# Stick-breaking attention: eight heads one by one, or four pairs of heads with two heads in an instruction

## The chip, the cores and the metric

The kernel runs on one core of one Trainium2 chip. TensorE (PE) multiplies, with its weight load (PEld) beside it; VectorE (DVE) and ScalarE (ACT) work on what it leaves in PSUM; GpSimd (POOL) and the DMA queues (SP's above all) do the rest. The metric is the device time of one execution in microseconds, the median of several.

## The reference

Two transformer blocks stand one behind the other, each on 512 tokens of width 1024. The first has stick-breaking attention and a gated recurrence side by side, and then a mixture of 16 experts; the second has retention, differential attention, cross attention and a feed-forward layer. The change touches the stick-breaking attention alone. It has 8 heads of width 64, and computes for a head

```
z           = (q k^T) / 8                                  # 512 queries x 512 keys
mask        = key position < query position
log_keep    = where(mask, log_sigmoid(-z), 0)
log_survive = reverse cumulative sum over keys of log_keep, shifted by one
a           = where(mask, exp(log_sigmoid(z) + log_survive), 0)
out         = a v
```

Since log_sigmoid(z) = z - softplus(z) and log_sigmoid(-z) = -softplus(z), the exponent is z minus the sum of softplus(z) over this key and all later keys that the query sees.

## The kernel before, in words

All wide products (a projection by a weight matrix) are made exact to fp32 by three products of rounded halves: `mm3` (L186 to L189) multiplies hi by hi, hi by lo and lo by hi. A weight tile of 512 KB comes in on SP's queue, ACT rounds it to `whi` (L169), DVE subtracts to `wlo` (L170), and 24 products of 128x512 make one output tile of 128 columns for all tokens. There are three buffers for the raw tile, and four for each half.

Scores are held transposed, keys on the partitions and queries along the row. A block j is 128 keys against the queries from 128 j on, so its width is n = 512, 384, 256 or 128 for j = 0 to 3. The head's steps (`sb_head`, L606) are: the score product of each block, plus a product of the identity with `negsb` that adds -1e30 where a query must not see the key (L615, L616); DVE copies the scores to `z` (L617); ACT makes exp(-|z|) and log(1 + that) in three passes, Abs, Exp and Ln (L619 to L621); DVE adds max(z, 0) (L622), which gives softplus; ACT and DVE split it into the halves `ph` and `pl` (L253, L254). Then, for each block, products with a triangle of ones (`tri`) and with all ones (`onesr`) over this block and the later ones give the sum over later keys (L633, L634); DVE subtracts it from z (L636), ACT takes the exponential (L637), and the product with the values goes into the head's half of `ysbp` (L638). ACT and DVE split that into `ysb`.

The q of a head stands in a tile of 128 partitions whose other 64 are zero, so that a score product runs over all 128 partitions. PSUM has eight banks: two of tag "mm" for the wide products, two of "tp", and four of "at", which scores and sums share. An fp32 product shows two records in the trace, a product of halves (fp32r) one.

A scheduler sets each engine's order when the kernel is built, and an engine then works strictly in that order. Around the eight heads it interleaves the wide products of the gates (16 tiles, L656 and L657, copied out by L653), which depend on the heads in nothing; their tiles share the 21 slots of `slp` with q, k and v, and five more (`GX`). After the last gate the branch products begin, the first of them with `ysb`.

Retention, in the second block, already has the form that the change gives to the attention here: `ret_pair` (L1256) multiplies the k and q of two heads on partitions 0 to 63 and 64 to 127 (L1266), and the values of two heads into the two halves of one PSUM tile (L1271).

Of the kernel before, what the change touches and what calls it, by code (L numbers as in the profile page):

```python
# [8 lines left out]
F32 = mybir.dt.float32  # L9
F32R = mybir.dt.float32r  # L10
# [3 lines left out]
AF = mybir.ActivationFunctionType  # L14
OP = mybir.AluOpType
AX = mybir.AxisListType.X
PSUM = bass.MemoryType.PSUM
# [3 lines left out]
S = 512  # L21
# [4 lines left out]
HID = 2816  # L26
CAP = 96
OVER = 10
NSL = 21
GX = (5, 6, 7, 8, 9)  # L30
NRX = 8
NRX2 = 12

# [50 lines left out]
def body(tc, a, out):  # L84
    nc = tc.nc
    V, A, T, G = nc.vector, nc.scalar, nc.tensor, nc.gpsimd
    es = ExitStack()

    def pool(name, bufs, side=None, space=None, stack=None):
        kw = {}  # L90
        if side:
            kw["side"] = side
        if space is not None:
            kw["space"] = space
        return (stack or es).enter_context(tc.tile_pool(name=name, bufs=bufs, **kw))
# [9 lines left out]
    hp = pool("hp", 1)  # L105
    ps = pool("ps", 1, space=PSUM)
    dp = pool("dp", 1, space=DRAM)

    def psum(tag, name="ps"):
        return ps.tile([128, 512], F32, name=name, tag=tag, bufs={"mm": 2, "at": 4, "tp": 2}[tag])  # L110

    def new_hT():
        return (hp.tile([128, 8, S], F32R, name="hTh"), hp.tile([128, 8, S], F32R, name="hTl"))
# [138 lines left out]
    def hilo(hi, lo, src):  # L252
        A.copy(hi, src)  # L253
        last_lo[:] = [V.tensor_sub(lo, src, hi.bitcast(F32))]  # L254
# [46 lines left out]

    def sums(tag, ones, *sq):
        w = sq[0].shape[1]
        m = psum(tag)[:, :w]
        for i, q in enumerate(sq):
            T.matmul(m, ones, q, start=(i == 0), stop=(i == len(sq) - 1))  # L306
        return m
# [91 lines left out]
    at = ExitStack()  # L399
    yp = pool("yp", 1, stack=at)  # L400
    yhg = [yp.tile([128, 4, S], F32R, name=f"yhg{i}") for i in range(2)]
    ysb = [yp.tile([128, 4, S], F32R, name=f"ysb{i}") for i in range(2)]
    slp = pool("slp", 1, stack=at)

    def slot(name):
        return slp.tile([128, S], F32, name=name, tag="sl", bufs=NSL)
# [165 lines left out]

    def ev_sq(t0):
        def f(t, o):
            for h in range(2):
                q = slot("sq")
                sq_[2 * (t0 + t) + h] = q
                G.memset(q[64 - 64 * h:128 - 64 * h, :], 0.0)
                A.activation(q[64 * h:64 * h + 64, :], o[64 * h:64 * h + 64, :], AF.Copy, scale=0.125)
        return f  # L580

    def ev_sk(t0):
# [13 lines left out]
        ws(w_in, 8, 512 + t * 128, 1, hT, S, ev_sk(t))  # L596
    hgst.close()

    slp2 = pool("slp2", 1, stack=at)
    sbst = ExitStack()  # L600
    sb = pool("sb", 1, side="right", stack=sbst)
    COL = [0, 512, 896, 1152, 1280]

    last_exp = []

    def sb_head(h):  # L606
        t = h // 2
        z = sb.tile([128, 1280], F32, name="z", bufs=2)
        ph = sb.tile([128, 1280], F32R, name="ph", bufs=2)
        pl = sb.tile([128, 1280], F32R, name="pl", bufs=2)  # L610
        for j in range(4):
            n = S - 128 * j
            cc = slice(COL[j], COL[j + 1])
            o = psum("at")[:, :n]
            T.matmul(o, sk_[t][:, j * 128:(j + 1) * 128], sq_[h][:, j * 128:], start=True, stop=False)  # L615
            T.matmul(o[:, :128], identb, negsb, start=False, stop=True)  # L616
            V.tensor_copy(z[:, cc], o)  # L617
            e = sb.tile([128, S], F32, name="ea", bufs=3)[:, :n]
            A.activation(e, o, AF.Abs)  # L619
            A.activation(e, e, AF.Exp, scale=-1.0)  # L620
            A.activation(e, e, AF.Ln, bias=onec)  # L621
            V.scalar_tensor_tensor(e, z[:, cc], 0.0, e, op0=OP.max, op1=OP.add)  # L622
            hilo(ph[:, cc], pl[:, cc], e)
        y = psum("tp", name="ysbp")
        for j in range(4):
            n = S - 128 * j
            cc = slice(COL[j], COL[j + 1])
            o = psum("at")[:, :n]
            for i in range(j, 4):
                m = tri if i == j else onesr  # L630
                ci = slice(COL[i], COL[i + 1])
                oo = o[:, (i - j) * 128:]
                T.matmul(oo, m, ph[:, ci], start=(i == j), stop=False)  # L633
                T.matmul(oo, m, pl[:, ci], start=False, stop=(i == 3))  # L634
            w = sb.tile([128, S], F32, name="ea", bufs=3)[:, :n]
            V.tensor_sub(w, z[:, cc], o)  # L636
            last_exp[:] = [A.activation(w, w, AF.Exp)]  # L637
            T.matmul(y[64 * (h % 2):64 * (h % 2) + 64, 128 * j:], sv_[j][:, h * 64:(h + 1) * 64], w,  # L638
                     start=(j == 0), stop=(j == 3))
        p0 = 64 * (h % 2)  # L640
        hilo(ysb[0][p0:p0 + 64, t, :], ysb[1][p0:p0 + 64, t, :], y[p0:p0 + 64, :])

    for h in range(8):
        sb_head(h)


    gt = {}

    def ev_gate(key):
        def f(t, o):  # L650
            n = t + (8 if key == "h" else 0)
            gt[key, t] = slot("gt") if n not in GX else slp2.tile([128, S], F32, name="gt2", bufs=len(GX))
            order(A.copy(gt[key, t], o), last_sk[0])  # L653
        return f

# [758 lines left out]
    ts(a["w_down_2"][0], NH, 0, 4, aT, ev_out(0), by_token=False, tag="at")  # L1414
    ts(a["w_down_2"][0], NH, 512, 4, aT, ev_out(512), by_token=False, tag=["mm", "mm", "tp", "tp"])
    fst.close()
    xp2.close()
    kvst.close()
    es.close()
# [25 lines left out]
```

## Time and profile before

| | |
|---|---|
| median of 3 runs | 1643.37 us (1640.85 to 1863.65) |
| profiled execution | 1641.05 us, span 1639.3 us |
| PE busy | 1602.2 us, 98% of the span |
| DVE, ACT busy | 960.2 us, 833.1 us |
| heads and gates, first score to first branch product | 231.6 to 391.2 us |

A busy time of PE is not the time that its work needs: a record of a 128x512 product lasts 0.39 us, while products that follow each other start 0.23 us apart. So the text counts from start to start. A row of the timeline merges products of one line that follow each other; its second number lasts to the end of the last, some 0.16 us after a product that follows would start (0.39 less 0.23). Numbers in brackets are idle time before an instruction, and what ended it.

### The profile page before, as it was taken

The page shows a single profiled execution, that of the slowest core. Times are in us where ns is not written, and L with a number is a line of the kernel's source. Part 1 is how long each engine was busy: PE and PEld are TensorE (multiplying, and loading weights), DVE is VectorE, ACT ScalarE, POOL GpSimd, SP SyncE. Part 2 cuts the span into 40 slices and gives each one's busy share as a digit, 9 for nine tenths or more (in the row PEclk, how much of TensorE's full clock was granted, in tenths as well). Part 3 has the DMA queues.
Part 4 walks back from the last instruction along what each step waited for, and adds up shares of the span by engine and source line. Part 5 has one row for each costly group of instructions (what it writes and reads, how often), then busy time and mean ns, then how long its engine had stood idle before and what let it go on. Part 6 is the DMA issues. An engine that isn't in the chain of part 4 may idle for free. (4 is left out here: it accounts for less than half of the span.)

```text
span 1639.3 us, 20501 instructions
## 1 busy us (share of the span) xinstructions
PE 1602.2 (98%) x7663; PEld 1234.2 (75%) x7663; DVE 960.2 (59%) x1533; ACT 833.1 (51%) x1331; POOL 74.6 (5%) x92
## 2 busy tenths in 40 slices
PE   7999999999999999999999999999999999999999
PEld 6887776678878777777677667558778888888887
DVE  6459945543647999999865656456654433333221
ACT  5445557565335888888765545425444423222120
POOL 3000000000001211110010000000000000000000
PEclk9999999999999999999999999999999999999999
DMA  7230121123479999999954213124311433333241
GB/s 230 66 103 27 57 82 30 52 93 101 141 244 328 342 370 362 368 361 364 371 192 136 64 52 91 45 71 128 91 52 52 116 103 91 103 91 103 91 128 39
DMA packets 203071, 242.89 MB, mean 148 GB/s; under 512 B 10400, under 2 KB 133560, under 8 KB 202968
## 3 DMA queue, kind: packets, MB, share of 16 engines
q1 hardware_dynamic: 188800, 205.43, 37.7%
q0 software_dynamic: 7056, 24.27, 5.3%
q10 hardware_dynamic: 7112, 11.85, 2.4%
q8 instruction: 61, 1.00, 0.2%
q14 instruction: 42, 0.34, 0.1%
HBM read 223.69 MB, written 15.73 MB: 146 GB/s over the span
## 5 line engine op out<-in xcount | busy, mean ns | idle before, releaser
L170 DVE TENSOR_TENSOR wlo<-wraw,whi 128x1024 fp32r<-128x1024 f32 x210 | 256.1, 1223 | 287.2 <-ACT whi L169 277.3
L169 ACT CAST whi<-wraw 128x1024 fp32r<-128x1024 f32 x210 | 220.5, 1051 | 387.6 <-PE ps L188 263.5
L187 PE MATMUL ps<-hTh,whi 128*128 128x512 f32 (+1 forms) x912 | 349.6, 384 | 1.3 <-DVE fsg L1396 0.8
L188 PE MATMUL ps<-hTl,whi 128*128 128x512 f32 (+1 forms) x912 | 348.2, 382 | 0.9 <-DVE hTl L254 0.9
L189 PE MATMUL ps<-hTh,wlo 128*128 128x512 f32 (+1 forms) x912 | 347.5, 381 | 0.0
L170 DVE TENSOR_TENSOR wlo<-rx,whi 128x1024 fp32r<-128x1024 f32 x176 | 210.8, 1221 | 33.9 <-ACT whi L169 32.6
L169 ACT CAST whi<-rx 128x1024 fp32r<-128x1024 f32 x176 | 183.2, 1049 | 51.6 <-PE ps L189 39.1
L187 PEld LDWEIGHTS ps<-hTh,whi 128*128 128x128 f32 x912 | 172.2, 189 | 34.1 <-issue 1.5
L188 PEld LDWEIGHTS ps<-hTl,whi 128*128 128x128 f32 x912 | 172.1, 189 | 33.3 <-issue 1.6
L189 PEld LDWEIGHTS ps<-hTh,wlo 128*128 128x128 f32 x912 | 172.1, 189 | 31.8 <-issue 0.9
L187 PE MATMUL ps<-whi,XT 128*96 128x512 f32 x256 | 102.0, 398 | 1.8 <-ACTq L1032 1.8
L189 PE MATMUL ps<-whi,XT 128*96 128x512 f32 x256 | 102.5, 400 | 0.0
L188 PE MATMUL ps<-wlo,XT 128*96 128x512 f32 x256 | 101.4, 396 | 0.0
L189 PE MATMUL ps<-whi,hTl 128*128 128x512 f32 x192 | 77.2, 402 | 0.0
L187 PE MATMUL ps<-whi,hTh 128*128 128x512 f32 x192 | 76.5, 398 | 0.3 <-ACT hTh L253 0.2
L188 PE MATMUL ps<-wlo,hTh 128*128 128x512 f32 x192 | 76.6, 399 | 0.0
L187 PE MATMUL ps<-whi,aTh 128*128 128x512 f32 x176 | 68.5, 389 | 0.0
L188 PE MATMUL ps<-wlo,aTh 128*128 128x512 f32 x176 | 68.5, 389 | 0.0
L189 PE MATMUL ps<-whi,aTl 128*128 128x512 f32 x176 | 68.5, 389 | 0.0
L1396 DVE TENSOR_TENSOR fsg<-fsg,ps 128x512 f32<-128x512 f32 x22 | 15.1, 688 | 76.0 <-PE ps L189 76.0
L187 PEld LDWEIGHTS ps<-whi,XT 128*96 128x96 f32 x256 | 41.7, 163 | 18.7 <-ACTq L1032 2.2
L188 PEld LDWEIGHTS ps<-wlo,XT 128*96 128x96 f32 x256 | 41.7, 163 | 17.4
(450 smaller groups left out, 2630.9 us busy)
## 6 DMA issues: line engine op xcount, KB each, us to landing
wraw<-in_w_in_dram SPq DMA_DIRECT2D x72, 512.0 KB
rx<-in_w_exp_gate_dram SPq DMA_DIRECT2D x58, 512.0 KB
rx<-in_w_exp_down_dram SPq DMA_DIRECT2D x58, 512.0 KB
rx<-in_w_exp_up_dram SPq DMA_DIRECT2D x52, 512.0 KB
wraw<-in_w_gate_dram SPq DMA_DIRECT2D x22, 512.0 KB
wraw<-in_w_up_dram SPq DMA_DIRECT2D x22, 512.0 KB
wraw<-in_w_down_dram SPq DMA_DIRECT2D x22, 512.0 KB
wraw<-in_w_out_dram SPq DMA_DIRECT2D x16, 512.0 KB
```

Source lines behind the costliest of these rows:

```text
L169: i1 = A.copy(hi, w)
L170: i2 = V.tensor_sub(lo, w, hi.bitcast(F32))
L187: T.matmul(o, lh, rh, start=first, stop=False)
L188: T.matmul(o, lh, rl, start=False, stop=False)
L189: T.matmul(o, ll, rh, start=False, stop=last)
L1396: V.tensor_mul(sg[t], sg[t], o)
```

## The change

Two heads go through each instruction of DVE and ACT: `sb_pair` takes the place of `sb_head`, four times. A tile of two PSUM banks holds one block of both heads, one bank for each (`psum2`): one such tile for the scores ("sc"), one for the sums ("run"). They take the four banks of "at" while the attention runs; `four_banks` opens and closes that pool. The zeros beside q are gone: a pair's q and k stand in one tile, and each head's score product runs over its own 64 partitions. The identity product with the mask is gone; DVE adds a mask from SBUF where it copied. The blocks go from the last to the first, and the sum of a block follows at once, since it needs this block and later ones only. The eight value products of a pair stand together at its end. The slots are 20, without the five extra ones.

```
--- before.py
+++ after.py
@@ -26,8 +26,7 @@
 HID = 2816
 CAP = 96
 OVER = 10
-NSL = 21
-GX = (5, 6, 7, 8, 9)
+NSL = 20
 NRX = 8
 NRX2 = 12
 
@@ -105,9 +104,22 @@
     hp = pool("hp", 1)
     ps = pool("ps", 1, space=PSUM)
     dp = pool("dp", 1, space=DRAM)
+    banks = [ExitStack(), None]
+
+    def four_banks(name, pairs=0):
+
+        banks[0].close()
+        banks[1] = (pool(name, 1, space=PSUM, stack=banks[0]), 4 - 2 * pairs, pairs)
+
+    four_banks("at0")
 
     def psum(tag, name="ps"):
-        return ps.tile([128, 512], F32, name=name, tag=tag, bufs={"mm": 2, "at": 4, "tp": 2}[tag])
+        if tag == "at":
+            return banks[1][0].tile([128, 512], F32, name=name, tag="at", bufs=banks[1][1])
+        return ps.tile([128, 512], F32, name=name, tag=tag, bufs=2)
+
+    def psum2(tag="at2"):
+        return banks[1][0].tile([128, 2, 512], F32, name=tag, tag=tag, bufs=banks[1][2])
 
     def new_hT():
         return (hp.tile([128, 8, S], F32R, name="hTh"), hp.tile([128, 8, S], F32R, name="hTl"))
...
@@ -401,6 +413,9 @@
     yhg = [yp.tile([128, 4, S], F32R, name=f"yhg{i}") for i in range(2)]
     ysb = [yp.tile([128, 4, S], F32R, name=f"ysb{i}") for i in range(2)]
     slp = pool("slp", 1, stack=at)
+    mask = yp.tile([128, S], F32, name="mask")
+    G.memset(mask[:, 128:], 0.0)
+    V.tensor_copy(mask[:, :128], negsb)
 
     def slot(name):
         return slp.tile([128, S], F32, name=name, tag="sl", bufs=NSL)
@@ -572,11 +587,8 @@
 
     def ev_sq(t0):
         def f(t, o):
-            for h in range(2):
-                q = slot("sq")
-                sq_[2 * (t0 + t) + h] = q
-                G.memset(q[64 - 64 * h:128 - 64 * h, :], 0.0)
-                A.activation(q[64 * h:64 * h + 64, :], o[64 * h:64 * h + 64, :], AF.Copy, scale=0.125)
+            sq_[t0 + t] = slot("sq")
+            A.activation(sq_[t0 + t], o, AF.Copy, scale=0.125)
         return f
 
     def ev_sk(t0):
@@ -596,60 +608,56 @@
         ws(w_in, 8, 512 + t * 128, 1, hT, S, ev_sk(t))
     hgst.close()
 
-    slp2 = pool("slp2", 1, stack=at)
     sbst = ExitStack()
     sb = pool("sb", 1, side="right", stack=sbst)
-    COL = [0, 512, 896, 1152, 1280]
-
+    four_banks("at1", 1)
+    hs = [slice(64 * h, 64 * h + 64) for h in range(2)]
     last_exp = []
 
-    def sb_head(h):
-        t = h // 2
-        z = sb.tile([128, 1280], F32, name="z", bufs=2)
-        ph = sb.tile([128, 1280], F32R, name="ph", bufs=2)
-        pl = sb.tile([128, 1280], F32R, name="pl", bufs=2)
-        for j in range(4):
-            n = S - 128 * j
-            cc = slice(COL[j], COL[j + 1])
-            o = psum("at")[:, :n]
-            T.matmul(o, sk_[t][:, j * 128:(j + 1) * 128], sq_[h][:, j * 128:], start=True, stop=False)
-            T.matmul(o[:, :128], identb, negsb, start=False, stop=True)
-            V.tensor_copy(z[:, cc], o)
-            e = sb.tile([128, S], F32, name="ea", bufs=3)[:, :n]
-            A.activation(e, o, AF.Abs)
+    def sb_pair(t):
+
+        y = psum("tp", name="ysbp")
+        z, ph, pl = {}, {}, {}
+        for j in (3, 2, 1, 0):
+            c0, n = 128 * j, S - 128 * j
+            o = psum2("sc")[:, :, :n]
+            for h in range(2):
+                T.matmul(o[:, h], sk_[t][hs[h], c0:c0 + 128], sq_[t][hs[h], c0:], start=True, stop=True)
+            z[j] = sb.tile([128, 2, n], F32, name=f"z{j}", bufs=2 if j > 1 else 1)
+            V.tensor_add(z[j], o, mask[:, None, :n].to_broadcast([128, 2, n]))
+            ph[j], pl[j] = (sb.tile([128, 2, n], F32R, name=f"p{q}{j}", bufs=2 if j > 1 else 1) for q in "hl")
+            e = sb.tile([128, 2, S], F32, name="ea", bufs=2)[:, :, :n]
+            A.activation(e, z[j], AF.Abs)
             A.activation(e, e, AF.Exp, scale=-1.0)
             A.activation(e, e, AF.Ln, bias=onec)
-            V.scalar_tensor_tensor(e, z[:, cc], 0.0, e, op0=OP.max, op1=OP.add)
-            hilo(ph[:, cc], pl[:, cc], e)
-        y = psum("tp", name="ysbp")
+            V.scalar_tensor_tensor(e, z[j], 0.0, e, op0=OP.max, op1=OP.add)
+            hilo(ph[j], pl[j], e)
+            o = psum2("run")[:, :, :n]
+            for h in range(2):
+                for i in range(j, 4):
+                    m = tri if i == j else onesr
+                    oo = o[:, h, (i - j) * 128:]
+                    T.matmul(oo, m, ph[i][:, h], start=(i == j), stop=False)
+                    T.matmul(oo, m, pl[i][:, h], start=False, stop=(i == 3))
+            V.tensor_sub(z[j], z[j], o)
+            last_exp[:] = [A.activation(z[j], z[j], AF.Exp)]
         for j in range(4):
-            n = S - 128 * j
-            cc = slice(COL[j], COL[j + 1])
-            o = psum("at")[:, :n]
-            for i in range(j, 4):
-                m = tri if i == j else onesr
-                ci = slice(COL[i], COL[i + 1])
-                oo = o[:, (i - j) * 128:]
-                T.matmul(oo, m, ph[:, ci], start=(i == j), stop=False)
-                T.matmul(oo, m, pl[:, ci], start=False, stop=(i == 3))
-            w = sb.tile([128, S], F32, name="ea", bufs=3)[:, :n]
-            V.tensor_sub(w, z[:, cc], o)
-            last_exp[:] = [A.activation(w, w, AF.Exp)]
-            T.matmul(y[64 * (h % 2):64 * (h % 2) + 64, 128 * j:], sv_[j][:, h * 64:(h + 1) * 64], w,
-                     start=(j == 0), stop=(j == 3))
-        p0 = 64 * (h % 2)
-        hilo(ysb[0][p0:p0 + 64, t, :], ysb[1][p0:p0 + 64, t, :], y[p0:p0 + 64, :])
-
-    for h in range(8):
-        sb_head(h)
+            for h in range(2):
+                T.matmul(y[hs[h], 128 * j:], sv_[j][:, (2 * t + h) * 64:(2 * t + h + 1) * 64], z[j][:, h],
+                         start=(j == 0), stop=(j == 3))
+        hilo(ysb[0][:, t, :], ysb[1][:, t, :], y)
+
+    for t in range(4):
+        sb_pair(t)
+
+    four_banks("at2")
 
 
     gt = {}
 
     def ev_gate(key):
         def f(t, o):
-            n = t + (8 if key == "h" else 0)
-            gt[key, t] = slot("gt") if n not in GX else slp2.tile([128, S], F32, name="gt2", bufs=len(GX))
+            gt[key, t] = slot("gt")
             order(A.copy(gt[key, t], o), last_sk[0])
         return f
 
...
```

PE's order around the end of a head before, where the next head's scores and the value products meet (L615 scores, L616 mask, L638 values; `sq` and `sk` are q and k, `ea` the weights, `sv` the values):

```order
L615 MATMUL ps<-sq,sk 128x512
L638 MATMUL ysbp<-ea,sv 64x512
L638 MATMUL ysbp<-ea,sv 64x384
L638 MATMUL ysbp<-ea,sv 64x256
L638 MATMUL ysbp<-ea,sv 64x128
L616 LDWEIGHTS identb
L616 MATMUL ps<-negsb,identb 128x128
L615 MATMUL ps<-sq,sk 128x384
```

PE's order of the change at the end of the second pair (L646 values, L640 and L641 sums, L625 scores; "x2" is one product of each head):

```order
L646 MATMUL ysbp<-z_2110,sv 64x384 x2
L646 MATMUL ysbp<-z_2085,sv 64x256 x2
L646 MATMUL ysbp<-z_2064,sv 64x128 x2
L640 MATMUL run<-ph_2206,tri 128x256
L641 MATMUL run<-pl_2207,tri 128x256
L640 MATMUL run<-ph_2185,onesr 128x128
L641 MATMUL run<-pl_2186,onesr 128x128
L640 MATMUL run<-ph_2206,tri 128x256
L641 MATMUL run<-pl_2207,tri 128x256
L640 MATMUL run<-ph_2185,onesr 128x128
L641 MATMUL run<-pl_2186,onesr 128x128
L625 MATMUL sc<-sq,sk 128x512 x2
```

The two heads' products now follow each other in the row, the value products come in one run, and the widest scores of a pair (here the third's) stand behind the values of the pair before it. From one such 512-wide score pair to the next (the second pair's and the third's) the order holds 28 wide products.

ACT's order of the change in the third pair, around the logarithm of its widest block (L632 Ln, L630 Abs, L631 Exp, L181 the rounding of a weight tile, L661 the copy of a gate, L643 the last exponential, L265 the rounding to `ph`; z_2302 and z_2323 are the fourth pair's first two blocks):

```order
L631 ACTIVATE ea<-ea 128x1024
L181 CAST whi<-wraw 128x1024
L632 ACTIVATE ea<-ea,onec 128x1024
L630 ACTIVATE ea<-z_2302 128x2x128
L661 COPY gt<-ps 128x512
L631 ACTIVATE ea<-ea 128x2x128
L632 ACTIVATE ea<-ea,onec 128x2x128
L643 ACTIVATE z_2229<-z_2229 128x768
L265 CAST ph_2260<-ea 128x1024
L265 CAST ph_2304<-ea 128x256
```

Five instructions, those of the next pair's block, of a gate and of the block before, stand between the logarithm of the widest block and its rounding. Of the 16 gates the order has 5 copied out before the last pair's values, where before it had 9; the wide products from the first score to the last value product are 135, and the other 254 of 389 up to the first branch product stand behind, in one row.

## Rows read from the trace of the kernel before

**Rows 1.** The page: busy us of the engines, share of the span, instructions.

```profile
PE 1602.2 (98%) x7663; PEld 1234.2 (75%) x7663; DVE 960.2 (59%) x1533; ACT 833.1 (51%) x1331; POOL 74.6 (5%) x92
```

**Rows 2.** Stretches: start:end, length, busy us (instructions) by engine, clock, DMA, GB/s.

```profile
231.60:391.20 159.60, 156.53 (x705) 111.17 (x704) 81.69 (x152) 102.26 (x217) 0.00 (x0) 1.00 0.21 67
1320.00:1560.00 240.00, 240.00 (x1060) 198.73 (x1059) 78.24 (x82) 66.76 (x82) 0.00 (x0) 1.00 0.32 97
```

**Rows 3.** SP's queue over the span, longest wait: total us, times, longest.

```profile
SPq L167 <- DVE wlo L170: 993.1, 168, 46.0
```

**Rows 4.** PE's timeline, one head's scores and masks: start, duration, instruction.

```profile
231.63 1.02 PE L615 MATMUL ps<-sq,sk 128*128 128x512 f32 x2
232.49 0.22 PE L616 MATMUL ps<-negsb,identb 128*128 128x128 bf16 x1
...
234.15 0.47 PE L187 MATMUL ps<-hTh,whi 128*128 128x512 f32 x1
```

**Rows 5.** PE's timeline, one head's value products.

```profile
245.74 2.37 PE L638 MATMUL ysbp<-ea,sv 128*64 128x512 f32 x8
```

**Rows 6.** PE's timeline, products of one head's sums.

```profile
253.93 0.39 PE L634 MATMUL ps<-pl,tri 128*128 128x512 f32 x1
254.16 0.34 PE L633 MATMUL ps<-ph,onesr 128*128 128x384 f32 x1
254.34 0.34 PE L633 MATMUL ps<-ph,tri 128*128 128x384 f32 x1
...
255.57 0.40 PE L633 MATMUL ps<-ph,onesr 128*128 128x256 f32 x2
...
257.03 0.28 PE L633 MATMUL ps<-ph,tri 128*128 128x128 f32 x1
```

**Rows 7.** PE's timeline, retention's pairs: scores L1266, values L1271.

```profile
1040.91 0.87 PE L1271 MATMUL ps<-pp,rv 128*64 128x384 f32 x4
...
1052.57 1.35 PE L1266 MATMUL ps<-rq,rk 64*128 64x384 f32 x8
...
1055.38 0.49 PE L1266 MATMUL ps<-rq,rk 64*128 64x128 f32 x4
1055.80 0.49 PE L188 MATMUL ps<-hTl,whi 128*128 128x512 f32 x1
1056.22 0.65 PE L1271 MATMUL ps<-pp,rv 128*64 128x256 f32 x4
...
1082.33 1.13 PE L1266 MATMUL ps<-rq,rk 64*128 64x512 f32 x4 [0.65 <-DVE rk L1253]
```

**Rows 8.** Groups of ACT, 231.6 to 391.2 us: count | busy, mean ns | idle before.

```profile
L169 ACT CAST whi<-wraw 128x1024 fp32r<-128x1024 f32 x17 | 17.8, 1048 | 12.7 <-PE ps L188 12.5
L653 ACT COPY gt<-ps 128x512 f32<-128x512 f32 x15 | 8.7, 580 | 7.7 <-PE ps L189 7.7
L621 ACT ACTIVATE ea<-ea,onec 128x512 f32<-128x512 f32 x8 | 5.7, 717 | 0.0
L620 ACT ACTIVATE ea<-ea 128x512 f32<-128x512 f32 x8 | 5.1, 632 | 0.1
L620 ACT ACTIVATE ea<-ea 128x256 f32<-128x256 f32 x8 | 3.4, 420 | 0.0
```

**Rows 9.** Groups of DVE, same stretch.

```profile
L170 DVE TENSOR_TENSOR wlo<-wraw,whi 128x1024 fp32r<-128x1024 f32 x16 | 19.6, 1225 | 31.8 <-ACT whi L169 31.8
L636 DVE TENSOR_TENSOR ea<-z,ps 128x512 f32<-128x512 f32 x8 | 5.5, 687 | 3.4 <-PE ps L634 3.4
```

**Rows 10.** PE's timeline at two idle gaps, and a stretch behind each.

```profile
528.74 0.47 PE L187 MATMUL ps<-whi,XT 128*96 128x512 f32 x1 [1.78 <-ACTq L1032]
...
843.38 0.33 PE L287 MATMUL ps<-ident,hn 128*128 128x128 f32 x1 [1.90 <-ACT mv L930]
...
529.20:532.50 3.30, 3.30 (x10) 2.10 (x9) 1.79 (x10) 1.95 (x2) 0.00 (x0) 0.50 0.68 221
843.40:846.80 3.40, 3.21 (x16) 2.28 (x17) 2.94 (x4) 3.14 (x5) 0.53 (x1) 1.00 0.91 276
```

More of the change, by code (lines that the diff above doesn't have):

```diff
@@ L303, in sums @@
         w = sq[0].shape[1]
-        m = psum(tag)[:, :w]
+        m = psum2()[:, 0, :w] if tag == "at2" else psum(tag)[:, :w]
         for i, q in enumerate(sq):
@@ L1416, in body @@
     fst.close()
+    banks[0].close()
     xp2.close()
```

## The prediction, made before the changed kernel ran

> **What bounds the kernel now.** The page comes first. PE is busy 98% of the span and no other engine comes near [rows 1]; but PE's busy time overlaps itself, so the next look is at starts. A stretch of nothing but 128x512 products holds 1060 of them in 240 us, 0.226 us each [rows 2]: PE at its pace. The reader is to see then who waits for whom: SP, which brings the weights, waits 993 us for DVE to free a raw buffer, which DVE does at the pace at which PE uses tiles [rows 3]. So PE's work and PE's waits set the end, and what the attention gives up or adds comes through whole. The profiled execution is 1641.05 us, 2.3 below the median of three (1643.37); my sum is made against the former.
>
> The stage is the stretch from the first score to the first branch product, 159.6 us [rows 2]. It holds 385 wide products, 87.2 us at 0.226. The heads have the other 72.4: scores with masks 2.52 us for a head (231.63 to 234.15) [rows 4], values 2.37 less the tail of 0.16, 2.2 [rows 5], and sums. A sum product takes 0.23 us at 512 columns, 0.18 at 384, (0.40 - 0.16) / 2 = 0.12 at 256, and 0.28 - 0.16 = 0.12 at 128 [rows 6]; a head has two each of 1, 2, 3 and 4 of these, 2.86 us. Eight heads make 20.2 + 17.6 + 22.9 = 60.7. What is left, 11.7 us, is waiting and switching.
>
> **The change, part by part.** *Scores.* Retention shows the new form. Two heads' 512-wide pair, four records, takes 1.13 - 0.16 = 0.97 us, the 384 and 256 together 1.35 - 0.16 = 1.19, the 128 0.33 [rows 7]: 2.49 us, about half of what two heads take in turn, so the two halves of the array work at once. Against it stands the switch: the wide product between two such groups takes 0.42 us (1055.80 to 1056.22) instead of 0.23 [rows 7], 0.2 for each visit. Four visits a pair: 3.3 us, 13.2 in all, with no masks, for 20.2 before.
>
> *Values.* 384 columns 0.87 - 0.16 = 0.71, 256 columns 0.49 [rows 7]; by columns 0.95 for 512 and 0.25 for 128. With one visit 2.6 us a pair, 10.4 for 17.6. *Sums* are the same products, 22.9.
>
> *PE's work* is then 13.2 + 10.4 + 22.9, with 389 wide products (four that stood ahead now stand in the stage) at 88.1: 134.6 us, against 159.6 + 0.9 = 160.5. If PE never waited, 26 us would go.
>
> *DVE and ACT.* A 1024-wide pass takes 1.22 us on DVE where two 512-wide ones take 2 x 0.69 [rows 9], on ACT 1.05 for 2 x 0.63 [rows 8]. The mask's addition replaces a copy; reading PSUM costs DVE no more than SBUF does here (0.687 at 512 wide, on the line of 1.22 at 1024) [rows 9], so it is free. The mask tile, the missing memsets and the full-width q copy lie beside the wide products ahead of the stage, whose order is nearly the same: nothing. Without that cover the copy into the mask, 128 wide, is under half a microsecond. The gates: 254 wide products now stand behind the heads, not beside them. That costs no work, but is cover withdrawn, and this decides the rest.
>
> *The new wait.* From one 512-wide score pair to the next the order makes a ring, since both engines work strictly in turn and each double tile exists once. Its steps: scores 0.97; DVE's addition 1.22; ACT's Abs and Exp, a weight cast between, and Ln, 3 x 1.05 + 1.14 (Ln 0.09 over Exp at 512) [rows 8]; on ACT the five that stand before the rounding, 0.42 + 0.58 + 0.42 + 0.51 + 0.84 = 2.77 (768 wide estimated as the mean of 512 and 1024), which hide DVE's 1.22; rounding 1.05; the low half 1.22; 15 of 16 sum products 2.37; then PE's nine wide products, four 128-wide sums and one product more, 2.75, which hide DVE's subtraction and ACT's exponential (2.27); values 2.6; eight sum products of the next pair 0.96. Together 20.2 us. PE's work in a ring is 3.3 + 2.6 + 5.7 + 28 x 0.226 = 17.9; ACT's 23 instructions there come to 17.3 by the same rows. So the ring binds, and PE's longest wait is for the rounding of the widest block.
>
> I take 21.5 for the ring: the sum leaves out four hand-overs from PE (0.16 each, the tail) and some of DVE's queue, whose 768-wide subtraction stands ahead of the widest block's softplus. Bounds: 17.9 below, if all waits are hidden, and 24.3 above, with another 768-wide and 1024-wide pass of each engine in series (0.84 + 1.05 + 0.95 + 1.22); 21.5 is nearest to the sum of rows. The heads take a start of 5 us (the first three score pairs, nine wide products and a part of the first block's chain), three rings, and an end of a ring less its last step: 5 + 64.5 + 20.5 = 90. Behind them 254 products, 57.5. The stage is 147.5 instead of 160.5: **13 us less, 1628 us**.
>
> The Trainium skill speaks against counting PE's work alone: TensorEngine Tiling (Array Packing), PSUM Bottleneck, says that packing makes TensorE faster but not the emptying of PSUM, which can become the limit. By PE's work alone the stage would be 134.6 us, by the ring 147.5; no row of before shows two heads in a ring.
>
> **The rivals.** *The clock falls.* With 17.9 of work in 21.5, PE stands still about 3.6 us in a ring, most of it in one piece. A gap of 1.78 us was followed by a stretch at 0.50, that is at 1.2 GHz, while behind one of 1.90 it stayed at 1.00 [rows 10]. Each 3.3 us at half the clock gives back 1.65; four or five of them, 7 to 8 us: 1635 to 1636. Against it: during the wait other work is due, and part of the loss falls into the next wait. The Trainium skill, TensorE: Matmul & The Clock Gate, HAM oscillation, describes this pattern: bursts of products with a wait between, where every burst starts at the lower clock. The two gaps say sometimes.
>
> *The two heads run in turn* and the tiling does nothing here. Scores would be 20.2 less 32 masks at 0.06 (0.22 - 0.16) [rows 4], 18.3, values 17.6; the ring grows by 0.97 and 1.8 to about 24.3; the heads take 5 + 4 x 24.3 - 1 = 101, the stage 158.7: 1639. Against it: retention's rows [rows 7].
>
> *Slower: the next pair is not hidden in the ring.* With one "sc" and one "run" tile, the next pair's first two blocks stand in the same queues; if their passes (ACT 5 x (0.42 + 0.63) = 5.3, DVE 4 x (0.42 + 0.69) = 4.4, less 1.4 that the ring counts already) lie in series, the ring is 28.5, the heads 118, the stage 175.5: 15 us more, 1656. It decides from a ring of 24.7 on. For it: ACT has 17.3 us of work in the ring, so little slack. Against it: the order issues those blocks' scores while ACT still works on the widest one.
>
> *No wait at all*: 1615, with the 26 us above.
>
> **The numbers.** Forecast 0.6, clock 0.18, in turn 0.05, slower 0.1, more than the forecast's best 0.07. The forecast's own range runs from a ring of 20.2 (1623) to one of 23 (1634). Leaving out the slower case's far part and the last case's, the range is 1619 to 1643. A change of 2% (33 us) is about what a measurement of this kernel can tell from none: faster than that is excluded by PE's work alone (26 us), but for something outside the stage, 0.03; slower needs a ring of 33, 0.03; within, 0.94.
>
> **What would show it.** In the profile after, the L625 pairs start a few ns apart and take about 1 us at 512 wide; the value run takes about 2.6. The 512-wide score pairs start 21 to 22 us apart. The stage from first score to first branch product is 146 to 150 us. PE's new idle time is before the sums of the widest block, ended by ACT's rounding, once in each ring; the row of wide products behind the heads has no gap. Wrong would be: rings over 24.7; score pairs in turn; several stretches at 0.5 within the heads; or a later stage that takes the gain back, by a longer wait of SP or of PE for weights.

## The result: 18 us less, 1625.6 us

The changed kernel takes **1625.63 us** (median of four runs, 1624.45 to 1626.00), the kernel before 1643.37 (median of three, 1640.85 to 1644.18). A fourth run of the kernel before, 1863.65 us, was in a slower state and is left out. The ratio is 0.9894, with a 95% interval of 0.9875 to 0.9914: a gain of 0.9 to 1.3%. The forecast was 1628, its range 1619 to 1643. The profiled execution took 1625.99 us, with a span of 1624.2 against 1639.3 before.

The page's line of busy time, which answers to [rows 1]:

```profile
PE 1585.2 (98%) x7631; PEld 1226.1 (75%) x7631; DVE 949.7 (58%) x1466; ACT 819.7 (50%) x1243; POOL 71.0 (4%) x85
```

PE's share is the same 98%, so the kernel is bound as before, and PE has 17 us less to do. DVE lost 67 instructions and 10.5 us, ACT 88 and 13.4; neither sets the end.

Three stretches of the changed kernel, with the columns of [rows 2]: the stage from the first score to the first branch product, its part behind the heads, and a piece of a later stage.

```profile
233.90:374.80 140.90, 136.96 (x673) 101.79 (x673) 72.06 (x84) 91.86 (x132) 0.00 (x0) 1.00 0.24 75
318.50:374.80 56.30, 56.30 (x249) 46.61 (x249) 12.94 (x11) 23.29 (x34) 0.00 (x0) 1.00 0.42 131
829.30:832.50 3.20, 3.20 (x8) 2.48 (x9) 2.67 (x4) 2.88 (x6) 0.00 (x0) 0.50 1.03 310
```

The stage is 141.0 us where it was 159.6 [rows 2]: 18.6 less, the whole of the gain. In it PE works at full clock (1.00, that is 2.4 GHz) and has 4 us without a product. Behind the heads 249 wide products run without a gap, 0.226 us each.

PE's timeline through the stage: start, duration, instruction, and in brackets the idle time ahead of it and what ended it.

```profile
233.87 0.49 PE L625 MATMUL sc<-sq,sk 64*128 64x128 f32 x4
...
239.13 1.13 PE L625 MATMUL sc<-sq,sk 64*128 64x512 f32 x4
...
249.53 0.50 PE L640 MATMUL run<-ph,tri 128*128 128x512 f32 x1 [0.53 <-ACT ph L265]
...
255.85 2.37 PE L646 MATMUL ysbp<-z,sv 128*64 128x512 f32 x16 [0.35 <-ACT z L643]
258.15 0.39 PE L640 MATMUL run<-ph,tri 128*128 128x256 f32 x1
...
259.22 1.13 PE L625 MATMUL sc<-sq,sk 64*128 64x512 f32 x4
...
278.92 1.13 PE L625 MATMUL sc<-sq,sk 64*128 64x512 f32 x4
...
299.58 1.13 PE L625 MATMUL sc<-sq,sk 64*128 64x512 f32 x4
...
318.27 0.50 PE L199 MATMUL ps<-hTh,whi 128*128 128x512 f32 x1
...
374.84 0.39 PE L199 MATMUL ps<-ysb,whi 128*128 128x512 f32 x1
```

A 512-wide score pair of both heads takes 1.13 us with its tail, where one head took 1.02 and a mask of 0.22 [rows 4]. The values of two heads, 16 records, take the 2.37 that one head's eight took [rows 5]. The 512-wide pairs start 20.1, 19.7 and 20.7 us apart.

The following table is summed from the same timeline: for each kind of product, the time from its start to the start of the next product on PE, over the whole stage. Such a sum has no overlaps, and its parts add up to the stage, but for rounding. A wait counts with the product ahead of it.

| us of the stage | before | after |
|---|---|---|
| scores and masks | 22.0 | 12.3 |
| values | 19.8 | 9.2 |
| sums | 25.2 | 25.6 |
| 384 wide products (86.9 at 0.2264) | 92.5 | 93.9 |
| stage | 159.6 | 141.0 |

Scores gave 9.7 us and values 10.6; the rest took 1.7 back. Waits were no large item in either kernel, as PE's waits among the heads show (waiting tile and line, releaser: us in total, times, longest; waits over 0.15 us), first of before, then of the change:

```profile
PE ysbp L638 <- ACT ea L637: 1.5, 3, 0.5
PE ps L615 <- DVE ea L636: 1.3, 5, 0.3
```

```profile
PE run L640 <- ACT ph L265: 2.7, 6, 0.5
PE ysbp L646 <- ACT z L643: 0.7, 2, 0.4
PE run L640 <- DVE z L642: 0.3, 1, 0.3
```

2.8 us before, 3.7 after (3.1 and 3.9 with the shorter ones), and the longest single one of the change is about half a microsecond. In the table 2.7 of the change's 3.9 lie with the wide products, 0.8 with the sums and 0.4 with the scores; of before's 3.1 half lie with the wide products and half with the sums.

Outside the stage the two executions drift by a few us. Wide product against wide product, the change is 1.55 us late at the start (PE's clock came up to full at 20.2 us, before at 17.1), 2.15 late when the attention begins, 16.4 ahead when it is over, 17.2 ahead at 504 us, and 15.1 at the end. One place where it loses again is a gap in a later stage:

```profile
827.92 1.14 PE L299 MATMUL ps<-ident,hn 128*128 128x128 f32 x8 [3.60 <-ACT mv L938]
```

The gap there was 1.90 us before, with the clock at 1.00 behind it [rows 10]; now it is 3.60, with 0.50 behind it (the third stretch above). That single profile is a low one of before (1641.05 against a median of 1643.37), which is most of why the medians differ by 17.7 us and the two profiled executions by 15.1. In a second profile of the changed kernel (run 9) PE's clock came up at 18.0 us, the stage began 1.2 us late, the gap was 3.62 us, and the span was 1622.0 us, 17.3 less than before.

### The profile page after: what moved, and what is told of

Its sections match the earlier page's. It is cut to its first block, busy times and chain, and to the rows that moved or that the text cites. A ratio compares the mean times of both kernels' runs of the same rounds, so it can differ in the third digit from the quotient of the medians.

```text
span 1624.2 us, 20208 instructions
## 1 busy us (share of the span) xinstructions
PE 1585.2 (98%) x7631; PEld 1226.1 (75%) x7631; DVE 949.7 (58%) x1466; ACT 819.7 (50%) x1243; POOL 71.0 (4%) x85
## 5 line engine op out<-in xcount | busy, mean ns | idle before, releaser
L181 ACT CAST whi<-wraw 128x1024 fp32r<-128x1024 f32 x210 | 220.6, 1052 | 403.4 <-PE ps L200 282.3
L181 ACT CAST whi<-rx 128x1024 fp32r<-128x1024 f32 x176 | 182.9, 1049 | 51.3 <-PE ps L201 36.2
L1404 DVE TENSOR_TENSOR fsg<-fsg,ps 128x512 f32<-128x512 f32 x22 | 15.1, 688 | 76.0 <-PE ps L201 76.0
L199 PEld LDWEIGHTS ps<-whi,XT 128*96 128x96 f32 x256 | 41.7, 163 | 18.7 <-ACTq L1040 2.2
L201 PEld LDWEIGHTS ps<-whi,XT 128*96 128x96 f32 x256 | 41.8, 163 | 17.3 <-issue 0.3
```

What stands on the lines that cost most here:

```text
L181: i1 = A.copy(hi, w)
L199: T.matmul(o, lh, rh, start=first, stop=False)
L201: T.matmul(o, ll, rh, start=False, stop=last)
```

## The experiments

Three theories were set against each other. **A**: the gain is TensorE's own work, since two heads' products run in two halves of the array at once. **B**: the gain comes from fewer and wider passes of DVE and ACT, that is from shorter waits. **C**: the ring from one pair's widest scores to the next is there, but the wide products fill it, so that its length matters little. A and B stood from the start; C was written down only for run 11, when the results of runs 1 to 8 were known. Run 4, say, is the experiment of that number. All times below are medians; the ratio is to the kernel before in the same comparison, and "stage" is the stretch from the first score to the first branch product in the profiled execution (141.0 for the change, 159.6 before).

**1. Scores in turn.** Both score products of a pair read the first head's partitions, so they use the same half of the array.

```
-  T.matmul(o[:, h], sk_[t][hs[h], c0:c0 + 128], sq_[t][hs[h], c0:], start=True, stop=True)
+  T.matmul(o[:, h], sk_[t][hs[0], c0:c0 + 128], sq_[t][hs[0], c0:], start=True, stop=True)
```

> Both score products of a pair read the rows of head 0 (head 1's scores are then head 0's), so that they lie in the same rows of TensorE's array and run in turn; all else stays, the order too. Theory A (the gain is TensorE's own work, the two halves of the array at once): the 16 score pairs take about 17 us instead of the 12.3 measured in the changed kernel's stage, and the time rises by 4 to 6 us over the changed kernel. Theory B (the gain is that DVE and ACT do two heads in one pass, so that TensorE waits less): the longer scores hide in waits, 0 to 1 us.

1629.22 us, ratio 0.9915 [0.9901, 0.9929]; stage 145.4, 4.4 more than the change. The widest pair on PE's timeline:

```profile
259.69 1.98 PE L625 MATMUL sc<-sq,sk 64*128 64x512 f32 x4
```

1.98 us where both halves took 1.13. Scores grow from 12.3 to 20.4 by starts; of these 8.0 us 3.6 are taken back, 2.8 in the wide products' share (93.9 to 91.1) and the rest in the sums'. Most of this is waiting, which falls from 3.9 to 1.3 us: PE waits less when it works longer. A holds for the scores, at about half of their own price, which was expected as 17 and not 20.4.

**2. Values in turn.** The loops of the value products change places, so that one head's four products follow each other and the halves no longer alternate. Nothing else is edited.

```
-  for j in range(4):
-      for h in range(2):
+  for h in range(2):
+      for j in range(4):
```

> The eight value products of a pair are written head by head (four of head 0, then four of head 1), so that products that follow each other lie in the same columns of the array and run in turn. Theory A: a run of values takes 4.4 us instead of 2.3, four runs 8.4 us more, and the time rises by 7 to 9 us. Theory B: 0 to 3 us, since waits of TensorE behind the values become shorter.

1632.0 us, ratio 0.9932 [0.9918, 0.9945]; stage 146.9, 5.95 more. The same run of 16 records:

```profile
255.67 3.93 PE L646 MATMUL ysbp<-z,sv 128*64 128x512 f32 x16 [0.35 <-ACT z L643]
```

3.93 for 2.37, four times 1.56: 6.2 us, where 8.4 were expected, and the stage shows nearly all of it. So 6.2 of the values' 10.6 us rest on the order of eight products alone. The other 4.4 stay with the halves in turn, and no run shows what gives them.

**3. One head for each instruction of DVE and ACT.** The tiles and PE's products stay, every pass of DVE and ACT is cut in two, and from Abs to the halves one head's passes come ahead of the other's.

```
-  A.activation(e, z[j], AF.Abs)
+  for h in range(2):
+      A.activation(e[:, h], z[j][:, h], AF.Abs)
...
```

> DVE and ACT get one instruction for each head, as in the kernel before; TensorE's products stay as changed. Theory A: TensorE's work is the same, so the time stays within 2 us of the changed kernel. Theory B: 16 blocks of 4 DVE and 5 ACT passes each pay a second start, 0.15 us on DVE (2 x 0.69 for 1.22) and 0.2 on ACT (2 x 0.63 for 1.05), up to 2.4 and 4 us for a pair, and the time rises by 6 to 12 us.

1633.34 us, ratio 0.9931 [0.9917, 0.9944]; stage 146.8, 5.9 more, though the rings are shorter (18.1, 17.9, 18.5): only 99 wide products stand among the heads, for 135. PE's timeline and waits:

```profile
250.90 0.91 PE L625 MATMUL sc<-sq,sk 64*128 64x384 f32 x2
251.74 0.50 PE L643 MATMUL run<-pl,tri 128*128 128x512 f32 x1
...
254.21 0.91 PE L625 MATMUL sc<-sq,sk 64*128 64x384 f32 x2
...
264.19 0.41 PE L642 MATMUL run<-ph,tri 128*128 128x384 f32 x1 [0.77 <-ACT z L646]
```

```profile
PE run L642 <- ACT z L646: 1.9, 3, 0.8
PE run L642 <- ACT ph L265: 1.5, 4, 0.7
```

Sums wait up to 0.8 us behind ACT's exponentials and roundings, but PE's waits together grow only from 3.9 to 4.3 us. The loss is in the products: scores go from 12.3 to 16.0 by starts, values from 9.2 to 10.8. In the order that the scheduler makes here 4 of the 16 score pairs are pulled apart, as the 384-wide one at 250.90 and 254.21 us, with sums between its halves. So the rise is near what B expected, but not by B's waits, and A's "same work" was wrong too: wide passes earn little of their own, but without them the pairs come apart and a third of the gain is lost.

**4. One more pass.** A multiplication by 1.0 on DVE in the chain of the widest block, which lengthens the ring and changes no value.

```
+  if j == 0:
+      V.tensor_scalar(e, e, 1.0, None, op0=OP.mult)
   hilo(ph[j], pl[j], e)
```

> The widest block of each pair gets one more DVE pass of 1.22 us (a multiplication by 1) between softplus and its rounding, on the ring from one widest score pair to the next. Theory A: rings grow from 20.1 to about 21.3 us, but the scheduler puts 158 wide products between the heads where 135 stood, and the time stays within 1 us. Theory B (the waits in the ring bind): 4 x 1.22, 4 to 5 us slower.

1624.9 us, ratio 0.989 [0.9875, 0.9905]; stage 140.3. PE's widest score pairs:

```profile
238.42 1.13 PE L625 MATMUL sc<-sq,sk 64*128 64x512 f32 x4
...
260.43 1.13 PE L625 MATMUL sc<-sq,sk 64*128 64x512 f32 x4
...
281.96 1.13 PE L625 MATMUL sc<-sq,sk 64*128 64x512 f32 x4
...
302.55 1.13 PE L625 MATMUL sc<-sq,sk 64*128 64x512 f32 x4
```

The rings are 22.0, 21.5 and 20.6, 1.2 longer on the mean, and cost nothing, as A expected: 158 wide products now stand among the heads.

**5. The mask alone, in the kernel before.** DVE adds the mask where it copied; the identity product goes, everything else stays as before.

```
-  T.matmul(o[:, :128], identb, negsb, start=False, stop=True)
-  V.tensor_copy(z[:, cc], o)
+  V.tensor_add(z[:, cc], o, mask[:, :n])
...
```

> The kernel before with one part of the change alone: no identity product with the mask; DVE adds a mask from SBUF where it copied, and ACT's Abs reads that result. Theory A (TensorE's own work): 32 products at 0.06 us go, 2 us less than before. Theory B (waits): Abs now stands behind DVE's addition, 0.7 us more in each of eight heads' chains, and the time stays or rises by up to 3 us.

1640.69 us, ratio 0.9978 [0.9969, 0.9986]; stage 155.5, 4.1 less than before. The masks themselves take 1.9 us by starts, and A expected 2. PE's waits fell by 1.3 us (3.1 to 1.8), and the order changed with them: 188 wide products stand among the heads, for 239. In the change the mask's part can thus be estimated as 2 to 4 of the 18.6.

**6. A short softplus.** The logarithm of 1 + exp z, without Abs and without the maximum: one pass fewer on each engine for every block.

```
-  A.activation(e, z[j], AF.Abs)
-  A.activation(e, e, AF.Exp, scale=-1.0)
+  A.activation(e, z[j], AF.Exp)
   A.activation(e, e, AF.Ln, bias=onec)
-  V.scalar_tensor_tensor(e, z[j], 0.0, e, op0=OP.max, op1=OP.add)
```

> The changed kernel with softplus as ln(1 + exp(z)): without the Abs pass on ACT and the pass of DVE that adds max(z, 0) (it holds for scores of this size; large ones would overflow). The ring from one widest score pair to the next loses 1.05 + 1.22 us or more. Theory A: TensorE's work stays, only its waits, some 6 us in the stage, can go: 0 to 3 us less, as the scheduler also puts only 95 wide products between the heads where 135 stood. Theory B: the waits bind, 5 to 7 us less.

1626.93 us, ratio 0.9898 [0.9883, 0.9912]; stage 141.7.

```profile
239.45 1.13 PE L625 MATMUL sc<-sq,sk 64*128 64x512 f32 x4
...
256.04 1.13 PE L625 MATMUL sc<-sq,sk 64*128 64x512 f32 x4
...
273.83 1.13 PE L625 MATMUL sc<-sq,sk 64*128 64x512 f32 x4
...
291.73 1.13 PE L625 MATMUL sc<-sq,sk 64*128 64x512 f32 x4
```

Rings of 16.6, 17.8 and 17.9, 2.7 shorter on the mean, and no gain: 95 wide products among the heads, and more of them behind. With run 4 this speaks against B: over this range the ring's length and the stage's are separate. A and C both allow it; run 11 sets those two apart.

**7. Blocks from first to last**, the sums in a loop of their own behind all scores.

```
-  for j in (3, 2, 1, 0):
+  for j in range(4):
...
+  for j in range(4):
+      n = S - 128 * j
       o = psum2("run")[:, :, :n]
```

> The changed kernel with the blocks in the order of the kernel before: the four blocks of a pair from first to last, all sums behind them. Theory A: TensorE's work is the same, and the scheduler puts 198 wide products between the heads where 135 stood: within 2 us of the changed kernel. Theory B: sums can't begin before the last block's softplus, so the chain of a pair is longer by the narrow blocks' passes (some 3 to 5 us) and the time rises by 4 us or more.

1634.2 us, ratio 0.9936 [0.9923, 0.9948]; stage 146.7, 5.7 more. PE's timeline at a widest pair:

```profile
245.23 1.12 PE L625 MATMUL sc<-sq,sk 64*128 64x512 f32 x2
246.28 0.44 PE L642 MATMUL run<-ph,onesr 128*128 128x384 f32 x1
246.65 1.12 PE L625 MATMUL sc<-sq,sk 64*128 64x512 f32 x2
```

In 6 of the 16 pairs the two heads' products no longer meet: here a sum product stands between them, and each takes its full 1.12. Scores go from 12.3 to 17.5 by starts, and values, now in four visits for each pair, from 9.2 to 11.0. 198 wide products are among the heads and PE's waits fall to 1.5 us, so cover isn't what is missing. B's size came true, but not its reason, the longer chain; A's "same work" was wrong. The change's order of blocks, with each sum behind its scores, keeps the pairs whole.

**8. Narrow sums joined.** For the two narrowest blocks both heads' sums stand side by side in one bank, so that one product does both: 24 products fewer (136 for 160; the 32 of the expectation is a miscount).

```
-  o = psum2("run")[:, :, :n]
-  for h in range(2):
+  o = psum2("run")
+  o = o[:, :, :n] if j < 2 else o[:, 0, :2 * n].rearrange("p (h m) -> p h m", h=2)
+  for h in range(2) if j < 2 else (slice(0, 2),):
```

> A try to be faster than both kernels: for the two narrow blocks (128 and 256 wide) the sums of both heads lie in one bank and one product makes both, 256 or 512 wide instead of two of 128 or 256; 32 of 160 sum products go. By the changed kernel's rows a 256-wide product takes 0.12 us and two 128-wide ones 0.17. Theory A: 0.3 to 0.4 us a pair, 1 to 2 us less than the changed kernel. Theory B: none, the waits take it.

1621.44 us, ratio 0.9856 [0.9841, 0.9870]; stage 138.1, 2.9 less than the change. PE's timeline at the sums of one pair's narrowest block, first of the change, then here:

```profile
254.94 0.22 PE L640 MATMUL run<-ph,tri 128*128 128x128 f32 x1
255.00 0.28 PE L641 MATMUL run<-pl,tri 128*128 128x128 f32 x1
255.11 0.28 PE L640 MATMUL run<-ph,tri 128*128 128x128 f32 x1
255.22 0.27 PE L641 MATMUL run<-pl,tri 128*128 128x128 f32 x1
```

```profile
255.78 0.28 PE L641 MATMUL run<-ph,tri 128*128 128x256 f32 x1
255.90 0.28 PE L642 MATMUL run<-pl,tri 128*128 128x256 f32 x1
256.02 0.39 PE L200 MATMUL ps<-hTl,whi 128*128 128x512 f32 x1
```

A 128-wide product costs up to 0.11 us, a 256-wide one 0.12, so two in one are nearly half the price. Sums fall from 25.6 to 22.7 by starts; 0.8 of these 2.9 are waits that followed them, 2.1 the products. PE's waits in the whole stage fall from 3.9 to 1.9 us, while scores and wide products, waits left out, take 1.2 us more; among the scores one 384-wide pair is pulled apart. So of the 2.9 net some 2.0 are waits, and what shortened them was not tried.

**9. The same again, beside the change**, on one chip in one comparison.

> The changed kernel once more, on the same chip as the three others, to compare with them: 17 to 19 us less than the kernel before.

> The kernel with the narrow sums of both heads in one product, beside the changed kernel on the same chip. Its stage was 2.8 us shorter; if that is TensorE's work (theory A), the time is 2 to 4 us below the changed kernel's here too.

The change: 1624.81 us, 20 less than before in this comparison where 17 to 19 was expected, ratio 0.9875 [0.9857, 0.9893], stage 140.99. Joined sums: 1622.18, 0.9856 [0.9839, 0.9873], stage 138.15. The stage repeats to 0.03 us, and is 2.84 shorter in both comparisons. The whole times differ by 2.6 us in the same direction, but their intervals overlap, so that a gain of the whole kernel isn't clear of the scatter of runs.

**10. Two blocks in one.** Beside the joined sums, the two narrowest blocks go as one piece of 384 columns for each head through the scores' tile, DVE and ACT: one visit and one chain fewer in each pair.

```
-  for j in (3, 2, 1, 0):
-      c0, n = 128 * j, S - 128 * j
+  for g in ((2, 3), (1,), (0,)):
+      n = sum(S - 128 * j for j in g)
...
```

> The kernel with joined narrow sums, and the two narrow blocks of a pair as one piece: one visit of TensorE for their scores, one pass of 768 on DVE and ACT for each that took two (256 and 512), save the subtraction. Theory A: four visits at 0.2 us less, 0.8 us, so 0 to 2 us below the kernel with joined sums alone. Theory B (waits): ACT and DVE save 5 x 0.2 and 3 x 0.15 us a pair, 4 to 6 us less.

1623.7 us, ratio 0.9867 [0.9849, 0.9885]; stage 137.9, against 138.15. Fewer passes again earn nothing that can be measured, now with 164 wide products among the heads.

**11. The bare ring.** The weights of the gates may be split only behind the last exponential, so that no wide product is left to stand among the heads.

```
-  ws(w_in, 8, 3584, 8, hT, S, ev_gate("s"))
-  ws(w_in, 8, 4608, 8, hT, S, ev_gate("h"))
+  ws(w_in, 8, 3584, 8, hT, S, ev_gate("s"), after=(last_exp[0], last_sub[0]))
+  ws(w_in, 8, 4608, 8, hT, S, ev_gate("h"), after=(last_exp[0], last_sub[0]))
```

> The changed kernel with all 384 wide products of the gates behind the heads (their weight casts are ordered behind the last exponential and the last subtraction). TensorE's work is the same. If that alone set the time (theory A), it would stay. If the ring is there and the wide products only fill it (theory C: the scheduler puts in as many as the ring leaves room for), the ring shows bare: some 18 us a pair without the gate's casts and products, heads of about 76 us, a stage of 76 + 87 = 163, and the time rises by 18 to 26 us.

1662.31 us, ratio 1.0106 [1.0089, 1.0123]: slower than the kernel before, and 37 us above the change (1624.81 in the same comparison). The direction is C's, but 18 to 26 was expected; the rings are 21.0, 20.5 and 18.4 us, not 18, and the expectation left out the clock. Its stage, three pieces of it, and the row of wide products behind the heads (columns as above):

```profile
233.60:406.90 173.30, 150.33 (x673) 113.17 (x673) 75.85 (x87) 97.47 (x135) 0.00 (x0) 0.90 0.23 70
238.20:248.40 10.20, 9.55 (x34) 6.42 (x34) 7.61 (x11) 9.44 (x15) 0.00 (x0) 0.50 0.00 0
255.00:265.00 10.00, 6.81 (x42) 3.75 (x43) 6.78 (x10) 7.80 (x11) 0.00 (x0) 1.00 0.00 0
303.20:313.20 10.00, 8.07 (x28) 7.05 (x27) 3.84 (x4) 3.54 (x4) 0.00 (x0) 0.50 0.00 0
319.50:406.90 87.40, 87.40 (x386) 72.41 (x385) 20.99 (x18) 35.37 (x48) 0.00 (x0) 1.00 0.45 138
```

Two of the waits ahead of these pieces:

```profile
236.09 0.92 PE L626 MATMUL sc<-sq,sk 64*128 64x384 f32 x4 [0.79 <-DVE z L628]
...
255.00 0.30 PE L641 MATMUL run<-ph,tri 128*128 128x128 f32 x1 [1.50 <-DVE z L643]
```

And PE's waits among the heads:

```profile
PE sc L626 <- DVE z L628: 6.1, 7, 1.3
PE run L641 <- DVE z L643: 5.9, 5, 1.5
PE ysbp L647 <- ACT z L644: 3.5, 4, 2.4
PE run L642 <- DVE pl L266: 3.4, 7, 0.9
PE run L641 <- ACT ph L265: 3.4, 1, 3.4
PE run L641 <- DVE z L628: 0.5, 1, 0.5
```

The stage is 32 us longer with the same products. PE waits 22.8 us among the heads where it waited 3.7: 19 of the 32. Waits left out, the products of the heads take 17 us more by starts, and the wide products, which now follow each other, 3.7 less; that is the other 13. A mean clock of 0.90 over 173.3 us means some 34 us at 0.50, that is 1.2 GHz. With PE busy 80 to 94% of such a stretch (8.07 of 10.00, 9.55 of 10.20) half of that, 14 to 16 us, would be lost to the clock: an estimate that accounts for most of the 17, though no run sets the clock apart from the changed order. So the cover that the wide products give is worth more than the change's whole gain, and a part of it is still enough (95 products in run 6).

## Why the prediction came true, and what in it was wrong

**The sign, the size and the main mechanism held.** The larger part of the gain is PE's own work in scores and values, by two halves of the array at once: taken out one at a time, they return 4.4 and 5.95 of the 18.6 us (runs 1 and 2). The mask's part is 2 to 4 (run 5). The 4 to 6 us that are left no run sets apart. The gain passes to the end of the kernel. By starts scores and values gave 20.3 us; the forecast had 13.2 for 20.2 and 10.4 for 17.6, which is 14.2. Each term was close: scores 13.2 forecast, 12.3 measured; values 10.4 and 9.2, for the run costs 2.30 us (255.85 to 258.15) and not 2.6; sums 22.9 and 25.6, of which 0.8 are waits behind them. Of the 6.1 us between 20.3 and 14.2, 4.0 come from the kernel before, which paid more around its scores and values than the rows of a single product tell (22.0 and 19.8 by starts, for 20.2 and 17.6).

**The step that was mis-sized is the wait**, "I take 21.5 for the ring". The sum of rows, 20.2, is what the trace has (20.1, 19.7, 20.7); the 1.3 us added for hand-overs and for DVE's queue were not there, three rings long. The end of the heads was 18.7 (299.58 to 318.27), not 20.5; the start 5.3, for 5. And 249 wide products stand behind the heads, not 254: the stage holds 384 of them, not 389, which is 1.1 us by itself. With 20.2 and 249 the prediction's own sum is 5 + 60.6 + 19.2 + 56.4 = 141.2, and measured are 141.0. Waits and switching together were forecast as 12.9 us (147.5 less 134.6); by the same prices they are 141.0 - 13.2 - 10.4 - 22.9 - 86.9 = 7.6. Only 3.9 of these are waits. The rest is work above its price: the wide products took 91.2 us without waits, not 86.9, and the sums 24.7, not 22.9, which scores and values gave back in part.

**The reason given for that term was wrong, and its number in part luck.** In the change's three rings PE stands still 1.4, 1.0 and 0.9 us; the other 18.7 to 19.8 us are its own products, priced as 17.9. "So the ring binds" would also mean that a longer ring costs and a shorter one gains. Run 4 lengthened it and run 6 shortened it, and the stage stayed within 0.8 us. What the ring holds of wide products moves with it (158, 135 and 95 among the heads in runs 4, the change and run 6), as it would if the scheduler places them where PE would wait. The 28 products for a ring that were read from the order are a result of the ring's length as much as a part of it. The three rings hold 23, 28 and 33. That the sum of rows came out right is therefore partly owed to the order already having been filled to that length.

**"PE stands still about 3.6 us in a ring, most of it in one piece" was wrong.** The place was right, before the sums of a block and ended by ACT's rounding, but six such waits make 2.7 us, and none is over 0.55. **The clock rival** did not come in: with such waits the clock is 1.00 through the stage. Its price is not imaginary: run 11, with single waits up to 3.4 us, has some 34 us at 0.50, in six stretches. The rule of the Trainium skill that was cited for this rival (TensorE: Matmul & The Clock Gate, HAM oscillation) fits run 11 in part: bursts with waits between them are there, but not every burst starts at the lower clock, for behind a wait of 1.50 us it stayed at 1.00. The rule does not describe the change.

**The rule that the emptying of PSUM becomes the limit** (the Trainium skill, TensorEngine Tiling (Array Packing), PSUM Bottleneck) shows here in run 11: with both products at once and nothing beside them, PE waits for DVE at the score tile 6.1 us and at the sum tile 5.9. With wide products between, none of these waits is in the change's list but one of 0.3.

**The other rivals.** *In turn*: excluded by the rows of runs 1 and 2, which show what that looks like. *The next pair not hidden*: no ring of the change came near its 24.7. *No wait at all* (1615): still 7.6 us of waits and switching. A part of this can be had, as run 8's stage of 138.1 shows, with fewer products and with 2.0 us less of waits.

**Given back later?** Hardly: of 18.6 us in the stage, 15 to 18 arrive. From the first branch product to the end the kernel before takes 1248.0 us and the two profiles of the change 1249.4 and 1248.1. The gap of 3.60 us that ACT's L938 ends, with the low clock behind it, is a part of this; it is there in both profiles (3.60 and 3.62), and why it grew was not tried and stays open. The later rise of the clock at the start is no effect of the change: it came at 20.2 and at 18.0 us in two executions of one kernel. Between 117 and 196 us, ahead of the stage, both profiles lose 0.6 us against before, where the forecast had nothing for the mask tile and the copies of q; which line costs it was not tried.

## What to carry to other kernels

Price a change of PE's work from start to start, over all kinds of products in the stage: that sum has no overlaps, shows what a kind of product costs with its switching, and adds up to the stage. Take the waits out first, since each falls to the kind of product ahead of it. A ring through several engines costs only what the order can't fill with independent products, so ask first how many such products are left to stand in it, and price the ring bare only where there are none. Products that use half the array gain only as neighbours: a single other product between them, or the wrong loop outside, takes the gain back.

## What was not expected of the hardware

- Two value products of 64 columns of the array each, writing different partitions of the same PSUM bank, run at once: 16 records in 2.37 us, in turn 3.93 (run 2). Two score products over 64 partitions each, to different banks: 1.13 and 1.98 (run 1).
- A 128-wide sum product starts its successor 0.06 to 0.11 us later, a 256-wide one 0.12 (run 8): two joined cost little more than one.
- The length of one gap didn't tell here whether the clock falls. Gaps up to 0.55 us in the change and one of 0.89 in run 10 left it at 1.00 all through the stage. In run 11 it fell to 0.50 at 238.2 us, behind gaps of 0.53, 0.79 and 0.32 us, while behind one of 1.50 at 255.0 it stayed at 1.00 for 10 us; behind one of 3.39 at 302.8 it was at 0.50 for 10 us.
